# Strassen products of an FFN input: two of four weight sums made by an adding transfer, with signs that turn all sums into additions

## The chip, the cores and the metric

The kernel runs on one core of a Trainium2 chip (trn2). The metric is the device time of one execution in microseconds. Five engines work side by side, each through its own queue in order: TensorE (PE; PEld is its weight load), VectorE (DVE), ScalarE (ACT), GpSimd (POOL) and SyncE (SP), which only issues transfers here.

## The reference

One inference step of a four-layer decoder for 512 prompt tokens and 8 sample tokens, held together as T = 520 columns of a model width of 1024. Each layer is a token mixer (sparse attention, chunked gating, linear recurrence, sparse attention) and then a dense SwiGLU network, both with a normalized residual:

```python
def swiglu_ffn(x, w_in, w_out):
    gate, up = jnp.split(x @ w_in, 2, axis=-1)
    return (jax.nn.silu(gate) * up) @ w_out
...
xp = deepnorm(xp, swiglu_ffn(xp, ffn_w_in[layer], ffn_w_out[layer]), ln_gain[layer, 1], ln_bias[layer, 1])
```

The hidden width is 2816 = 22 blocks of 128; each block has a gate part and an up part in w_in. Everything is float32.

## The kernel before, in words

**Matrix products.** x lies transposed in SBUF, 128 rows by 8 blocks (k) by 520 columns. A float32 product is made of three passes with split operands: each operand is rounded to a high part H (a CAST on ScalarE) and the residue is kept as L (a subtraction, mostly on VectorE); TensorE adds H x H, L x H and H x L into one PSUM bank. For weights `Weights.split` does this: the cast at L145, the residue at L147. A step of `Weights` is one such split of a 128 x 512 piece. `need` keeps the steps five ahead of the product that asks for one (`ahead`), and with `lag` set, as in the FFN, a residue is issued only with the next step's cast. Engines run strictly in the order in which the kernel issues their instructions.

**The FFN.** The 22 hidden blocks are taken in three chunks of 8, 7 and 7 (`CH`). In `ffn_body` the first 3 blocks of the first chunk are plain products (`mm`, L330 to L332); the other 5, and all of the next chunks, are Strassen pairs. After each chunk `out_proj` multiplies the gated hidden rows by w_out.

**A Strassen pair.** A pair is the gate block and the up block of one hidden block: A11 and A12 are the two halves of the gate weights (k 0 to 3 and 4 to 7), A21 and A22 those of the up weights. B11 to B22 are the corresponding quarters of x (260 columns each). Seven products of 12 matmuls (`prod`, L523 to L525) replace eight:

```python
PRODUCTS = (("A11", "B11", 0), ("S1", "T1", 1), ("S2", "T2", 3), ("A12", "B21", 4), ("S4", "B22", 5),
            ("S3", "T3", 6), ("A22", "T4", 9))
```

The third number places the product in the order of all pairs of the chunk, seven apart from pair to pair. The sums of a pair are S1 = A21 + A22, S2 = S1 - A11, S3 = A11 - A21, S4 = A12 - S2. All four run on GpSimd (`sum`: S1 at L170, S2 at L172, S3 at L174, S4 at L176), four steps ahead of the split that reads them (`SUMLEAD`), into five rotating buffers called fsum.

**The other side.** `right` makes T1 = B12 - B11, T2 = B22 - T1, T3 = B22 - B12 and T4 = B21 - T2 once per layer, in two halves (j = 0, 1), all at L502: T1 and T2 on VectorE, T3 and T4 on GpSimd. Each is then split by `Net.split` (L291 cast, L292 residue). They share the fsum buffers with the weight sums. This happens while TensorE still runs the plain products.

**Taking the products apart.** `gated` collects the seven products in three PSUM banks per pair (x: products 0, 2, 5, 6; y: 1, 4; z: 3). Products 0, 1, 2 and 5 are copied out by ScalarE (L570), and a later product into the same bank waits for that copy. VectorE adds 3 and 4 (L573, L576) and multiplies 6 (L583); GpSimd adds and multiplies the up part (L579, L580; in a chunk's last pair VectorE does); ScalarE applies SiLU (L550) and casts (L555), VectorE takes the residue (L556).

**Transfers.** SP loads each pair with two transfers of 512 KB (`dma`, L131), as soon as slots of the common pool of 39 (g) come free, at most some steps ahead. The normalization before the FFN (`ln`) ends with eight tensor_scalar of GpSimd per half of the columns (L397) and the residues L353 of VectorE that wait for them. It runs while TensorE is in the plain products, and its GpSimd instructions are issued between the first weight sums.

## Time and profile before

| what | us |
|---|---|
| median of 3 runs | 3063.47 (3060.45 to 3068.73) |
| the profiled execution, its time | 3060.67 |
| the profiled execution, its span | 3059.0 |
| TensorE busy | 2798.2 |
| VectorE busy | 2201.5 |
| ScalarE busy | 1538.7 |
| GpSimd busy | 1106.8 |

The profile is that of one execution. Busy times are sums over the span; a row of the trace gives an instruction's start, length, engine, source line, operation and tiles (out<-in), and in brackets how long its engine had idled before it and what ended that. Matmuls overlap each other, so what one costs is the distance of two starts, not the length of one. PEclk is the share of the full TensorE clock that was granted.

### The profile page before, as it was taken

To read this page: it belongs to the slowest core of one execution; us is meant where nothing else is said; L and a number is where in the kernel's file an instruction comes from. 1 tells how busy PE (TensorE), PEld (TensorE's weight loads), DVE (VectorE), ACT (ScalarE), POOL (GpSimd) and SP (SyncE) were. 2 spreads that over 40 slices of the span, in tenths; PEclk is the share of its full clock that TensorE was granted. 3 is DMA by queue.
4 is the path that set the end of the run, shared out by engine and by line. 5 is a ranking of instruction groups with operands and counts; after the bars stand their busy time and mean duration, and the time that the engine had idled before them with its cause. 6 is when DMAs were issued, how large, how long until landed. Compare 5 with 4: busy or idle time off the path is not lost.

```text
span 3059.0 us, 56135 instructions
## 1 busy us (share of the span) xinstructions
PE 2798.2 (91%) x21818; PEld 2663.7 (87%) x21818; DVE 2201.5 (72%) x4197; ACT 1538.7 (50%) x3466; POOL 1106.8 (36%) x894
## 2 busy tenths in 40 slices
PE   7999888999989889998899898999899988889997
PEld 7888578999989889998899888999898876889997
DVE  4788656686856786687677677587768877575885
ACT  4666544454445453464445445354456665353543
POOL 0222144364431454354222226355312222353562
PEclk9999999999999999999999999999999999999999
DMA  4222541333323032341212221332322144313321
GB/s 173 65 61 83 162 141 50 97 98 103 97 77 111 29 97 83 103 133 63 78 57 78 71 98 56 98 103 88 115 85 65 58 126 153 108 59 102 96 94 53
DMA packets 136044, 280.59 MB, mean 92 GB/s; under 512 B 13026, under 2 KB 76002, under 8 KB 135778
## 3 DMA queue, kind: packets, MB, share of 16 engines
q1 hardware_dynamic: 127168, 261.86, 26.9%
q10 hardware_dynamic: 7458, 10.95, 1.0%
q0 software_dynamic: 1152, 4.19, 0.5%
q8 instruction: 172, 2.82, 0.4%
q14 instruction: 94, 0.77, 0.1%
HBM read 263.69 MB, written 13.27 MB: 91 GB/s over the span
## 4 chain that ended last, share of the span: by engine, by line
PE 58%; DVE 16%; ACT 7%; issue 3%; POOL 3%; DMA 1%; SPq 0%; ACTq 0%; POOLq 0%; DVEq 0%
PE ps L330 9%; PE ps L332 9%; PE ps L331 9%; PE ps L523 8%; PE ps L525 7%; PE ps L524 7%; DVE g L147 3%; DVE row L375 2%; POOL x L397 2%; PE ps L846 1%; DVE x L366 1%; ACT g L291 1%; DVE g L828 1%; DVE g L292 1%; ACT g L1155 1%
## 5 line engine op out<-in xcount | busy, mean ns | idle before, releaser
L330 PE MATMUL ps<-g 128*128 128x256 f32 (+1 forms) x3744 | 1100.4, 294 | 21.4 <-ACT g L145 13.9
L331 PE MATMUL ps<-g 128*128 128x256 f32 (+1 forms) x3744 | 1073.1, 287 | 23.3 <-DVE g L147 20.6
L332 PE MATMUL ps<-g 128*128 128x256 f32 (+1 forms) x3744 | 1073.3, 287 | 2.9 <-DVE g L353 1.6
L330 PEld LDWEIGHTS ps<-g 128*128 128x128 f32 x3744 | 723.9, 193 | 34.7 <-ACT g L145 14.1
L331 PEld LDWEIGHTS ps<-g 128*128 128x128 f32 x3744 | 723.1, 193 | 31.6 <-DVE g L147 22.8
L332 PEld LDWEIGHTS ps<-g 128*128 128x128 f32 x3744 | 720.6, 192 | 4.3 <-DVE g L292 2.3
L523 PE MATMUL ps<-g 128*128 128x260 f32 x2128 | 608.6, 286 | 47.2 <-ACT frow L570 47.2
L524 PE MATMUL ps<-g 128*128 128x260 f32 x2128 | 604.6, 284 | 0.0
L525 PE MATMUL ps<-g 128*128 128x260 f32 x2128 | 604.2, 284 | 0.0
L147 DVE TENSOR_TENSOR g<-g 128x512 fp32r<-128x512 f32 (+1 forms) x632 | 497.3, 806 | 79.8 <-ACT g L145 79.0
L145 ACT CAST g<-g 128x512 fp32r<-128x512 f32 (+1 forms) x712 | 418.6, 610 | 156.7 <-PE ps L332 111.1
L523 PEld LDWEIGHTS ps<-g 128*128 128x128 f32 x2128 | 404.5, 190 | 53.8 <-ACT frow L570 53.8
L524 PEld LDWEIGHTS ps<-g 128*128 128x128 f32 x2128 | 404.9, 190 | 0.0
L525 PEld LDWEIGHTS ps<-g 128*128 128x128 f32 x2128 | 404.8, 190 | 0.0
L147 DVE TENSOR_TENSOR g<-fsum,g 128x512 fp32r<-128x512 f32 x304 | 346.4, 1157 | 23.6 <-ACT g L145 20.0
L145 ACT CAST g<-fsum 128x512 fp32r<-128x512 f32 x304 | 189.0, 623 | 56.9 <-PE ps L332 48.7
L1155 ACT ACTIVATE g<-g,nst 128x128 f32<-128x128 f32 (+3 forms) x256 | 143.4, 561 | 120.5 <-DVE nst L1153 118.5
L1167 POOL TENSOR_SCALAR g<-g,nst 128x128 f32<-128x128 f32 (+3 forms) x64 | 76.4, 1194 | 344.1 <-DVE nst L1160 236.4
L147 POOL TENSOR_TENSOR g<-g 128x512 fp32r<-128x512 f32 x80 | 105.7, 1327 | 250.4 <-ACT g L145 244.5
L170 POOL TENSOR_TENSOR fsum<-g 128x512 f32<-128x512 f32 x76 | 120.8, 1590 | 148.3 <-DMA g<-ffn_in 129.5
L172 POOL TENSOR_TENSOR fsum<-fsum,g 128x512 f32<-128x512 f32 x76 | 123.8, 1629 | 127.3 <-issue 126.1
L570 ACT COPY frow<-ps 128x260 f32<-128x260 f32 x304 | 113.7, 374 | 110.3 <-PE ps L525 110.3
(268 smaller groups left out, 4341.8 us busy)
## 6 DMA issues: line engine op xcount, KB each, us to landing
g<-ffn_in SPq DMA_DIRECT2D x176, 512.0 KB, 4.1
g<-ffn_out SPq DMA_DIRECT2D x64, 448.0 KB, 3.3
g<-nsa_in SPq DMA_DIRECT2D x42, 512.0 KB, 4.2
cm<-cache_cmp SPq DMA_DIRECT2D x64, 256.0 KB, 3.7
g<-cache_slc SPq DMA_DIRECT2D x128, 128.0 KB, 2.4
g<-cache_win SPq DMA_DIRECT2D x32, 512.0 KB, 4.8
...
```

The lines of the kernel that those rows point to most:

```text
L145: self.nc.scalar.copy(h, src)
L147: self.subs.append(lambda: (eng or self.nc.vector).tensor_sub(l, src, h.bitcast(FT)))
L170: g.tensor_add(t, q(2, 1), q(2, 2))
L172: g.tensor_sub(t, self.sums[i, "S1"], q(1, 1))
L330: nc.tensor.matmul(p[:, :n], H[:, s], a, start=k == 0, stop=False)
L331: nc.tensor.matmul(p[:, :n], L[:, s], a, start=False, stop=False)
L332: nc.tensor.matmul(p[:, :n], H[:, s], b, start=False, stop=k == nk - 1)
L523: nc.tensor.matmul(p, H[:, s], a, start=start and k == 0, stop=False, skip_group_check=True)
L524: nc.tensor.matmul(p, L[:, s], a, start=False, stop=False, skip_group_check=True)
L525: nc.tensor.matmul(p, H[:, s], b, start=False, stop=k == 3, skip_group_check=True)
L570: nc.scalar.copy(s[q], p)
L1155: defer(lambda P=P, i=i: (self.table(LN_EXP), nc.scalar.activation(P, P, AF.Exp, bias=st[:, i:i + 1], scale=-1.0, accum_out=st[:, 4 + i:5 ...
```

## The change

Four things, all in the FFN input.

1. **Signs.** T1, T2 and T4 are now B11 - B12, -(T1 + B22) and -(T2 + B21); T3 stays. The weight sums become S1 = A21 + A22, S3 = A21 + A11, S2 = S1 + A11 and S4 = S2 + A12 in the terms of the new layout: the up weights lie first in memory, then the gate weights, which gives quarters 0 to 3 = (A21, A22, A11, A12) of one row of 2048 numbers. The host's arrangement of ffn_w_in changes accordingly; the signs that differ are taken up where the products come out (L577 with scale -1 for products 1 and 5, a factor -1 for product 6).
2. **S1 and S3 by transfers.** `begin` at "D" lets SP load quarter 0 (A21) twice, side by side, into one slot. At "add" GpSimd issues a transfer that adds quarters 1 and 2 (A22, A11) onto it. The halves of the slot then are S1 and S3. "A1" loads quarters 2 and 3 (A11, A12) and "A22" loads quarter 1 again, into an fsum buffer.
3. **S2 and S4** stay on GpSimd, as additions (L180).
4. **T2 and T4** become SCALAR_TENSOR_TENSOR on VectorE; T4 thereby leaves GpSimd.

The lead of each part, in steps, is in LEADS: the load D is issued 12 steps ahead of S1's split, the addition 7, A1 6 ahead of A11's, A22 5, S2 and S4 3. Lines from `Weights` on move by 6 or 7 (L502 becomes L503 to L509, L523 to L525 become L530 to L532, L570 becomes L577, L579 and L580 become L586 and L587).

```diff
--- before.py
+++ after.py
@@ -39,7 +39,8 @@
 
 PRODUCTS = (("A11", "B11", 0), ("S1", "T1", 1), ("S2", "T2", 3), ("A12", "B21", 4), ("S4", "B22", 5),
             ("S3", "T3", 6), ("A22", "T4", 9))
-SUMLEAD = 4
+
+LEADS = (("D", "S1", 12), ("add", "S1", 7), ("A1", "A11", 6), ("S2", "S2", 3), ("S4", "S4", 3), ("A22", "A22", 5))
 HALF = T // 2
 
 
@@ -87,7 +88,8 @@
 
     def __init__(self, net):
         self.net, self.nc = net, net.nc
-        self.items, self.raw, self.ready, self.sums = [], {}, {}, {}
+        self.items, self.raw, self.ready = [], {}, {}
+        self.pairs, self.got = [], {}
         self.steps, self.pos, self.first, self.early = [], {}, [], {}
         self.nd = self.n = 0
         self.rawn, self.ahead = 3, 5
@@ -107,18 +109,16 @@
 
     def plan_pairs(self, pairs):
 
-        i0 = len(self.items)
-        self.items += pairs
+
+        i0 = len(self.pairs)
+        self.pairs += pairs
         for n, q in products(len(pairs)):
-            key = i0 + n, PRODUCTS[q][0]
+            key = ("p", i0 + n), PRODUCTS[q][0]
             self.add(key, lambda key=key: self.factor(*key))
-        for i in range(i0, len(self.items)):
-            for x in ("S1", "S2", "S4", "S3"):
-                at = self.pos[i, x] - SUMLEAD
-                self.early.setdefault(at, []).append((i, x))
-                if x == "S1":
-                    self.first.append(at)
-        return list(range(i0, len(self.items)))
+        for i in range(i0, len(self.pairs)):
+            for x, of, lead in LEADS:
+                self.early.setdefault(max(0, self.pos[("p", i), of] - lead), []).append((i, x))
+        return [("p", i) for i in range(i0, len(self.pairs))]
 
     def add(self, key, f):
         self.pos[key] = len(self.steps)
@@ -158,36 +158,36 @@
         n = self.items[i][0].shape[1]
         self.split((i, p), self.taken(i)[0][:, 512 * p:min(n, 512 * p + 512)], self.sub[p])
 
...
+
+    def begin(self, i, x):
+
+        nc, ap, t = self.nc, self.pairs[i], self.got.setdefault(i, {})
+        if x == "D":
+            d = self.net.flat(FT)[:, :1024]
+            nc.sync.dma_start(d.rearrange("p (a b) -> p a b", a=2), ap[:, None, :512].to_broadcast([128, 2, 512]))
+            t["S1"], t["S3"], t["D"] = d[:, :512], d[:, 512:], d
+        elif x == "add":
+            nc.gpsimd.dma_start(t["D"], ap[:, 512:1536], accum_op=OP.add)
+        elif x == "A1":
+            r = self.net.flat(FT)[:, :1024]
+            nc.sync.dma_start(r, ap[:, 1024:])
+            t["A11"], t["A12"] = r[:, :512], r[:, 512:]
+        elif x == "A22":
+            t[x] = self.net.fsum()
+            nc.sync.dma_start(t[x], ap[:, 512:1024])
         else:
...
+            t[x] = self.net.fsum()
+            p, q = ("S1", "A11") if x == "S2" else ("S2", "A12")
+            nc.gpsimd.tensor_add(t[x], t[p], t[q])
+
+    def factor(self, u, name):
+        self.split((u, name), self.got[u[1]][name], None)
 
     def need(self, *key):
 
         lim = min(len(self.steps), self.pos[key] + 1 + self.ahead)
         while self.n < lim:
             for x in self.early.pop(self.n, ()):
-                self.sum(*x)
+                self.begin(*x)
             self.steps[self.n][1]()
             self.n += 1
         if self.n == len(self.steps):
@@ -476,9 +476,10 @@
         u, j0 = [], 0
         f = lambda ap: ap.rearrange("p k c -> p (k c)")
         for c, n in enumerate(CH):
-            pairs = [tuple(f(a["ffn_in"][layer, j, s]) for s in range(2)) for j in range(j0, j0 + n)]
+            pairs = [a["ffn_in"][layer, j].rearrange("p s k c -> p (s k c)") for j in range(j0, j0 + n)]
             m = PLAIN if c == 0 else 0
-            u.append((self.W.plan([x for pair in pairs[:m] for x in pair]), self.W.plan_pairs(pairs[m:])))
+            plain = [x[:, s:s + 1024] for x in pairs[:m] for s in (1024, 0)]
+            u.append((self.W.plan(plain), self.W.plan_pairs(pairs[m:])))
             u.append(self.W.plan([f(a["ffn_out"][layer, m, :, j0:j0 + n]) for m in range(8)]))
             j0 += n
         return u
@@ -489,17 +490,23 @@
     def right(self, X, B):
 
 
-        nc = self.nc
+        v, g = self.nc.vector, self.nc.gpsimd
         x = lambda r, c, j: self.x[:, 4 * r - 4 + 2 * j:4 * r - 2 + 2 * j, HALF * (c - 1):HALF * c]
         for n in ("T1", "T2", "T3", "T4"):
             B[n] = [self.flat(FR)[:, :4 * HALF].rearrange("p (k t) -> p k t", k=4) for _ in range(2)]
         for j in range(2):
             t = {}
-            for n, o, p, q in (("T1", nc.vector, x(1, 2, j), x(1, 1, j)), ("T2", nc.vector, x(2, 2, j), "T1"),
-                               ("T3", nc.gpsimd, x(2, 2, j), x(1, 2, j)), ("T4", nc.gpsimd, x(2, 1, j), "T2")):
+            for n in ("T1", "T2", "T3", "T4"):
                 t[n] = self.fp.tile([128, HALF * 2], FT, name="fsum", tag="fsum", bufs=5).rearrange(
                     "p (k t) -> p k t", k=2)
-                o.tensor_sub(t[n], t.get(p, p) if isinstance(p, str) else p, t[q] if isinstance(q, str) else q)
+                if n == "T1":
+                    v.tensor_sub(t[n], x(1, 1, j), x(1, 2, j))
+                elif n == "T2":
+                    v.scalar_tensor_tensor(t[n], t["T1"], -1.0, x(2, 2, j), op0=OP.mult, op1=OP.subtract)
+                elif n == "T3":
+                    g.tensor_sub(t[n], x(2, 2, j), x(1, 2, j))
+                else:
+                    v.scalar_tensor_tensor(t[n], t["T2"], -1.0, x(2, 1, j), op0=OP.mult, op1=OP.subtract)
                 self.split(B[n][0][:, 2 * j:2 * j + 2], B[n][1][:, 2 * j:2 * j + 2], t[n])
                 yield
         for r, c in ((1, 1), (2, 1), (2, 2)):
@@ -567,7 +574,7 @@
             run_due()
             if q in (0, 1, 2, 5):
                 s[q] = self.frow()
-                nc.scalar.copy(s[q], p)
+                nc.scalar.activation(s[q], p, AF.Copy, scale=-1.0 if q in (1, 5) else 1.0)
             eng = nc.vector if last else nc.gpsimd
             if q == 3:
                 nc.vector.tensor_add(s[0], s[0], p)
@@ -580,7 +587,7 @@
                 defer(2, lambda s=s, e=eng: e.tensor_mul(s[1], s[1], s[2]))
                 put(3, j, 1, s[1])
             elif q == 6:
-                nc.vector.tensor_mul(s[0], s[0], p)
+                nc.vector.scalar_tensor_tensor(s[0], p, -1.0, s[0], op0=OP.mult, op1=OP.mult)
                 put(1, j, 0, s[0])
         while due:
             run_due()
@@ -1530,7 +1537,8 @@
     g = np.concatenate([i["ln_gain"].reshape(8, 8, 128), i["gmlp_ln_v"][:, 0].reshape(1, 8, 128)], 0)
     b = np.concatenate([i["ln_bias"].reshape(8, 8, 128), i["gmlp_ln_v"][:, 1].reshape(1, 8, 128)], 0)
     o["ln_gb"] = np.stack([g, b], 1).transpose(3, 0, 1, 2)
-    o["ffn_in"] = i["ffn_w_in"].reshape(DEPTH, 8, 128, 2, NFF, 128).transpose(0, 4, 3, 2, 1, 5)
+    o["ffn_in"] = i["ffn_w_in"].reshape(DEPTH, 8, 128, 2, NFF, 128)[:, :, :, ::-1].transpose(
+        0, 4, 2, 3, 1, 5)
     o["ffn_out"] = i["ffn_w_out"].reshape(DEPTH, NFF, 128, 8, 128).transpose(0, 3, 2, 1, 4)
     blocks = lambda w: w.reshape(8, 128, -1, 128).transpose(2, 1, 0, 3)
     o["gmlp_in"], o["gmlp_out"] = blocks(i["gmlp_w_in"][0]), blocks(i["gmlp_w_out"][0])
```

On GpSimd, in mid-stretch, in the seven-product rhythm of one pair. Before (fsum is a weight sum, frow an evicted product):

```order
L170 TENSOR_TENSOR fsum<-g 128x512
L579 TENSOR_TENSOR frow<-frow 128x260
L172 TENSOR_TENSOR fsum<-fsum,g 128x512
L580 TENSOR_TENSOR frow<-frow 128x260
L176 TENSOR_TENSOR fsum<-g,fsum 128x512
L174 TENSOR_TENSOR fsum<-g 128x512
```

And now:

```order
L180 TENSOR_TENSOR fsum<-g 128x512
L169 DMA g<-ffn_in 128x1024
L180 TENSOR_TENSOR fsum<-fsum,g 128x512
L586 TENSOR_TENSOR frow<-frow 128x260
L587 TENSOR_TENSOR frow<-frow 128x260
```

Four sums became two, and the adding transfer (L169) of the next pair stands between S2 and S4 of this one.

On VectorE, in one pass of `right` (g<-fsum is the residue of a T). Before:

```order
L502 TENSOR_TENSOR fsum<-x 128x520
L292 TENSOR_TENSOR g<-fsum,g 128x520
L502 TENSOR_TENSOR fsum<-x,fsum 128x520
L292 TENSOR_TENSOR g<-fsum,g 128x520 x3
L617 TENSOR_TENSOR row<-row,ps 128x264
```

And now:

```order
L503 TENSOR_TENSOR fsum<-x 128x520
L292 TENSOR_TENSOR g<-fsum,g 128x520
L505 SCALAR_TENSOR_TENSOR fsum<-fsum,x 128x520
L292 TENSOR_TENSOR g<-fsum,g 128x520 x2
L509 SCALAR_TENSOR_TENSOR fsum<-fsum,x 128x520
L292 TENSOR_TENSOR g<-fsum,g 128x520
L624 TENSOR_TENSOR row<-row,ps 128x264
```

T4 (L509) now stands on VectorE between the residue of T3 and its own.

On GpSimd at the start of a layer's FFN, among the last instructions of the normalization (L397). Before:

```order
L170 TENSOR_TENSOR fsum<-g 128x512
L172 TENSOR_TENSOR fsum<-fsum,g 128x512
L397 TENSOR_SCALAR x<-x,lngn,lngb 128x264 x8
L176 TENSOR_TENSOR fsum<-g,fsum 128x512
L174 TENSOR_TENSOR fsum<-g 128x512
L170 TENSOR_TENSOR fsum<-g 128x512
L502 TENSOR_TENSOR fsum<-x 128x520
L502 TENSOR_TENSOR fsum<-x,fsum 128x520
```

And now:

```order
L169 DMA g<-ffn_in 128x1024
L397 TENSOR_SCALAR x<-x,lngn,lngb 128x264 x4
L180 TENSOR_TENSOR fsum<-g 128x512
L397 TENSOR_SCALAR x<-x,lngn,lngb 128x264 x4
L169 DMA g<-ffn_in 128x1024
L180 TENSOR_TENSOR fsum<-fsum,g 128x512
L507 TENSOR_TENSOR fsum<-x 128x520 x2
```

The first pair's S2 stands between the two halves of the eight L397, and T4 is gone from this queue; only the two T3 (L507) are left of `right`.

## Rows read from the trace of the kernel before

**Rows 1.** The page, part 1: busy time, share of the span, instructions.

```profile
PE 2798.2 (91%) x21818; PEld 2663.7 (87%) x21818; DVE 2201.5 (72%) x4197; ACT 1538.7 (50%) x3466; POOL 1106.8 (36%) x894
```

**Rows 2.** The page, part 4: the chain that ended last, by engine.

```profile
PE 58%; DVE 16%; ACT 7%; issue 3%; POOL 3%; DMA 1%; SPq 0%; ACTq 0%; POOLq 0%; DVEq 0%
```

**Rows 3.** Windows: length, busy PE, PEld, DVE, ACT, POOL (count), clock, DMA share, GB/s.

```profile
620.00:640.00 20.00, 20.00 (x169) 20.00 (x168) 15.86 (x21) 12.67 (x30) 12.46 (x10) 1.00 0.34 116
650.00:670.00 20.00, 19.46 (x162) 19.25 (x162) 19.93 (x21) 10.47 (x26) 16.51 (x12) 1.00 0.18 51
```

**Rows 4.** Timeline of TensorE, the three restarts in the stretch from 617.7 to 691.0.

```profile
660.12 0.39 PE L523 MATMUL ps<-g 128*128 128x260 f32 x1 [0.54 <-ACT frow L570]
...
671.19 0.39 PE L523 MATMUL ps<-g 128*128 128x260 f32 x1 [0.72 <-ACT frow L570]
...
689.27 0.39 PE L523 MATMUL ps<-g 128*128 128x260 f32 x1 [0.52 <-ACT frow L570]
```

**Rows 5.** Groups from 649.08 to 671.2: count, busy us, mean ns, idle before.

```profile
L147 DVE TENSOR_TENSOR g<-fsum,g 128x512 fp32r<-128x512 f32 x8 | 10.5, 1330 | 0.1
...
L170 POOL TENSOR_TENSOR fsum<-g 128x512 f32<-128x512 f32 x2 | 3.5, 1736 | 0.0
L174 POOL TENSOR_TENSOR fsum<-g 128x512 f32<-128x512 f32 x2 | 2.9, 1471 | 0.0
```

**Rows 6.** Timeline of VectorE at 648 us, where GpSimd idles.

```profile
647.87 0.41 DVE L576 TENSOR_TENSOR frow<-frow,ps 128x260 f32<-128x260 f32 x1
648.21 0.68 DVE L147 TENSOR_TENSOR g<-fsum,g 128x512 fp32r<-128x512 f32 x1
```

**Rows 7.** Waits of TensorE over the span: us, times, longest.

```profile
PE ps L523 <- ACT frow L570: 47.2, 32, 9.3
```

**Rows 8.** Timeline of VectorE, GpSimd and TensorE before layer 0's 5-pair stretch.

```profile
499.46 0.70 DVE L502 TENSOR_TENSOR fsum<-x 128x520 f32<-128x520 f32 x1
...
507.09 0.70 DVE L292 TENSOR_TENSOR g<-fsum,g 128x520 fp32r<-128x520 f32 x1 [2.08 <-ACT g L291]
...
508.96 0.69 DVE L502 TENSOR_TENSOR fsum<-x 128x520 f32<-128x520 f32 x1
510.35 0.70 DVE L292 TENSOR_TENSOR g<-fsum,g 128x520 fp32r<-128x520 f32 x1 [0.69 <-ACT g L291]
...
512.36 2.18 DVE L292 TENSOR_TENSOR g<-fsum,g 128x520 fp32r<-128x520 f32 x2 [0.70 <-ACT g L291]
516.60 1.21 DVE L292 TENSOR_TENSOR g<-fsum,g 128x520 fp32r<-128x520 f32 x1 [2.05 <-ACT g L291]
...
514.62 1.28 POOL L502 TENSOR_TENSOR fsum<-x,fsum 128x520 f32<-128x520 f32 x1 [1.48 <-DVE g L292]
...
521.13 0.58 PE L523 MATMUL ps<-g 128*128 128x260 f32 x1 [6.57 <-ACT frow L570]
```

**Rows 9.** Tile hgrn_state, loads of 512 KB that GpSimd issues: time to landing.

```profile
DMA to landing us min/median/max: 4.3/5.5/7.1
```

**Rows 10.** Timeline of GpSimd and VectorE at one such issue.

```profile
1471.60 0.93 POOL L925 DMA_DIRECT2D g<-hgrn_state  x1 [8.34 <-ACT g L145]
...
1471.53 0.69 DVE L147 TENSOR_TENSOR g<-g 128x512 fp32r<-128x512 f32 x1
```

**Rows 11.** Lines 432 and 434, plain and signed form: ns min/median/max.

```profile
L432 DVE TENSOR_TENSOR row<-row x34: 415/428/806, 449.9 to 3049.6; 128x256 f32<-128x256 f32 x17, 128x264 f32<-128x264 f32 x17
...
L434 DVE SCALAR_TENSOR_TENSOR row<-row x34: 418/426/434, 450.4 to 3050.0; 128x256 f32<-128x256 f32 x17, 128x264 f32<-128x264 f32 x17
```

**Rows 12.** Windows behind the pauses of 3.20 and of 6.57 us; columns as above.

```profile
491.20:497.00 5.80, 5.80 (x35) 5.80 (x36) 4.92 (x5) 3.50 (x8) 4.76 (x4) 0.71 0.02 4
521.10:531.00 9.90, 9.87 (x63) 9.87 (x64) 7.46 (x10) 5.01 (x12) 4.40 (x4) 0.74 0.17 50
```

**Rows 13.** Timeline of GpSimd and TensorE at the normalization's end in layer 0.

```profile
487.62 3.95 POOL L397 TENSOR_SCALAR x<-x,lngn,lngb 128x264 f32<-128x264 f32 x4 [0.39 <-ACT g L393]
...
491.19 0.39 PE L331 MATMUL ps<-g 128*128 128x256 f32 x1 [3.20 <-DVE g L147]
```

19 lines of the change are left out of this document (removed).

## Prediction

> **What bounds the kernel now.** I read the page first: TensorE is busy 91% of the span, VectorE 72%, GpSimd 36% [rows 1], and the chain that ended last is 58% TensorE, 16% VectorE and 3% GpSimd [rows 2]. So time is to be had only where TensorE stands still, and the change touches only the stretches of the Strassen products. There are 12: per layer one of 5 pairs and two of 7. A pair is 7 products of 12 matmuls, 84 in all.
>
> Next I laid two windows of 20 us in one 7-pair stretch side by side [rows 3]. In the early one TensorE starts 169 matmuls, one per 0.12 us, and VectorE is busy 15.86 us; in the later one TensorE starts 162 and VectorE is busy 19.93 us. A pair costs TensorE 84 x 0.12 = 10.08 us. Late in the stretch TensorE stands still twice, and restarts at 660.12 and 671.19 [rows 4]: the period of a pair is 11.07 us there, and VectorE is busy through all of it. VectorE sets the pace once the lead of the first pairs is eaten. TensorE idles 0.54 and 0.72 us for ScalarE's copy L570, which comes late because ScalarE first waits for VectorE's eviction L573. The third wait, 0.52 us at 689.27, is of another sort: in the last pair the product with S3 is followed at once by the one with A22 in the same bank, and the copy lies between them.
>
> Why VectorE is late shows in the groups of two such periods [rows 5]: the residue L147 of a sum takes 1330 ns on average. Where GpSimd idles the same instruction takes 0.68 us, and an eviction before it 0.41 us, of which 0.07 overlaps with what follows [rows 6]. So, undisturbed, a pair would cost VectorE 7 residues x 0.61 + 5 operations of the eviction's width (L573, L576, L583, twice L556) x 0.34 = 5.97 us. The other 11.07 - 5.97 = 5.1 us fall on GpSimd's work, 16.51 us in 20 [rows 3], that is 9.1 per period: 0.56 us of VectorE per us of GpSimd.
>
> Last I took all waits of TensorE on L570: 47.2 us in 32 waits, the longest 9.3 [rows 7]. The 24 in the eight 7-pair stretches, 1.8 us a stretch as in [rows 4], make 14.4; some 32 us lie in the four 5-pair stretches, nearly all of it at one place, before the first product with S2 (6.57 us in layer 0 [rows 8]).
>
> **The change part by part.**
>
> *Two sums fewer on GpSimd.* S1 and S3 (L170 and L174, 1.74 + 1.47 us [rows 5]) become the work of a transfer. GpSimd keeps 9.1 - 3.2 = 5.9 us per pair, which at 0.56 cost VectorE 3.3 us: a pair takes it 5.97 + 3.3 = 9.3 us, or 9.8 if issuing the adding transfer (0.93 us [rows 10]) disturbs it like a sum. The bounds 5.97 and 9.8 both lie under TensorE's 10.08. So the two waits in mid-stretch go; next in line is TensorE itself. Each costs its idle time, plus 0.16 (a matmul is drawn 0.28 long but starts every 0.12), plus 0.11 (the one that restarts is drawn 0.39): 0.54 + 0.72 + 0.54 = 1.8 us per 7-pair stretch, in eight of them **-14.4 us**. The third wait stays.
>
> *T4 from GpSimd to VectorE.* Ahead of the 5-pair stretch VectorE and ScalarE work through T1 to T4 twice [rows 8]. The first pass runs from 499.46 to 507.09 + 0.70 = 507.79, 8.33 us; the second from 508.96 to 516.60 + 1.21 = 517.81, 8.85. GpSimd's T4 starts only when VectorE has finished T3's residue, and its 1.28 us lie in the chain. Afterwards GpSimd makes only T3, from x alone, which I take to be ready in time. From T1 to T2's residue 3.40 us remain (512.36 - 508.96). Then come the residues of T2 and T3, 2 x 0.63; T4 and its cast until its residue starts, 1.39 like T1's (510.35 - 508.96), since the signed form costs what the plain one does (426 against 428 ns, [rows 11]); and that residue, 0.70: 6.75 us. Saved are 1.6 + 2.1 = 3.7 us per layer. The tail from there to TensorE's restart at 521.13 is untouched, so TensorE restarts that much sooner: **-15 us** over four layers.
>
> *The clock behind that pause.* After the 6.57 us the granted clock averages 0.74 over 9.9 us, a mix of its two levels, 1.2 and 2.4 GHz: 2.6 us lost. After a pause of 3.20 us it is 0.71 over 5.8 us: 1.7 lost [rows 12]. The pause that remains is 6.57 - 3.7 = 2.9 us, so I take the nearer row: **-3.6 us** over four layers. Bounds: 0 and, with no loss left, -10.4.
>
> *S2 of the first pair, moved on GpSimd.* It now stands between the two halves of the eight L397. The later half started at 487.62 after 0.39 us of idling [rows 13], so it comes 1.28 - 0.39 = 0.9 us later (a sum like T4's 1.28). TensorE's 3.20 us pause there, behind an L147 that stands behind the L353 that waits for L397, grows as much. I price it at nothing: the T chain, not TensorE, decides the restart. Without that cover it costs 4 us over the layers.
>
> *The transfers.* SP issues three per pair instead of two, GpSimd one; 1.75 MB land instead of 1, so the DMA share of 0.34 [rows 3] would become some 0.6. D, A1 and A22 are issued pairs (over 10 us) ahead of their use and hide. SP's new wait, for a free sum buffer, holds up the next D and A1, which have that lead too. On GpSimd the adding transfer waits for D, and the next S2 waits until the addition has landed; S4, L579 and L580 are queued behind, and ScalarE's casts wait for them. A round there is landing + a sum 1.74 + issue 0.93. The trace has no adding transfer. Copies issued by GpSimd land in 4.3 to 7.1 us, median 5.5 [rows 9]. Lower bound 5.5, a copy; upper bound 11, twice that, since source and destination are both read. I take 7.1, the slowest copy: a round of 9.8, under 10.08, no cost.
> A rule speaks against this transfer: by the Trainium skill, SBUF — State Buffer, section "SBUF: two separate sides", GpSimd cannot write a transfer's descriptors while VectorE runs a two-port copy, and one of about 0.62 us became 3.1. With 2.5 us more on a landing of 5.5 a round would be 10.7 us, an estimate; over five rounds that is 3 us, within the lead worked out below, so the sum would stay. The trace does not show such a stall: an issue took 0.93 us while VectorE ran a residue, which kept its 0.69 [rows 10].
>
> *Signs.* L570 gets a scale and L583 a factor, with the same operands and widths: no cost [rows 11].
>
> **Sum.** -14.4 - 15 - 3.6 = -33. The profiled execution took 3060.67 us, 2.8 under the median of the runs, 3063.47. That makes 3027.7 on its scale and 3030.5 on the median's. Forecast: **3030 us**, its own range 3018 to 3042.
>
> **Rivals.**
> 1. *The additions land late*, and the change ends slower. With 11 us a round is 13.7, 3.6 us over TensorE's pair. A 7-pair stretch has five such rounds, 18 us, of which some 5 are covered (weights are prepared five products, 7.2 us, ahead; cast and residue take 2): 13 lost instead of 1.8. A 5-pair one has three: 11 less 5, 6 lost against 4.6 won. Together 8 x 11.2 + 4 x 1.4 = +95: 3158. It turns into a loss from about 9 us of landing. For it: no row has such a transfer; against it: the copies' rows. 0.10.
> 2. *VectorE stays over 10.08 us*, because the issue holds it or GpSimd's remaining work costs it more: only the T chain's 18.6 us are won, 3045. 0.12.
> 3. *The starting pause stays*, behind T3 or something else, and the longer pause of the normalization is paid: -14.4 + 4, 3053. 0.10.
> 4. *Nothing moves*: 2 and 3 together, 3063. For it: GpSimd is 3% of the chain. 0.08.
>
> **Chances.** The forecast has 0.60. A measurement of this kernel can tell 0.3%, 9 us, from no change. Faster: forecast, 2 and 3, 0.82. Same: 4, 0.08. Slower: 1, 0.10. The range leaves out 1 and 4 (0.18). It reaches from the whole clock loss won back and two more us per layer, 3014, to rival 3, 3053.
>
> **What would show it.** Right: a late window of 20 us in a 7-pair stretch holds 167 to 169 matmuls, with VectorE clearly under 20 us; L147 on a sum is under 1.0 us; TensorE's waits on the copy are about 0.5 us per 7-pair stretch and some 3 at the start of a 5-pair one; T1 to T4's residue takes near 6.7 us, twice. Wrong: GpSimd waits of several us for the transfer, landings of 9 us or more, or VectorE still full.

## The result and the profile after

| | before | after |
|---|---|---|
| median, us | 3061.96 (3058.99 to 3068.73, 4 runs) | 3026.73 (3025.43 to 3028.20, 4 runs) |
| span of the profiled execution, us | 3059.0 | 3024.5 |

The ratio is 0.9882 (95% interval 0.9864 to 0.9900). The medians lie 35 us apart, forecast 33. The time is inside the likeliest case's own range. Of the three terms, the profile bears out the one of GpSimd's sums with its cause, and that of the clock in its sum only. The third, the move of T4, has about the right sum for a reason that the runs refute.

The page, part 1, and the chain by engine. VectorE lost 169 us of work and GpSimd 220 [rows 1], and TensorE now holds 69% of the chain instead of 58% [rows 2]:

```profile
PE 2796.2 (92%) x21818; PEld 2663.4 (88%) x21818; DVE 2032.7 (67%) x4205; ACT 1554.8 (51%) x3466; POOL 887.0 (29%) x810
...
PE 69%; DVE 16%; ACT 7%; issue 3%; DMA 2%; POOL 2%; SPq 1%; ACTq 0%; POOLq 0%; DVEq 0%
```

Two windows late in a 7-pair stretch, and the groups of two pairs there (columns as in [rows 3, 5]):

```profile
640.00:660.00 20.00, 20.00 (x169) 20.00 (x168) 15.70 (x25) 13.31 (x31) 11.51 (x10) 1.00 0.62 143
650.00:670.00 20.00, 20.00 (x170) 20.00 (x169) 15.42 (x25) 13.71 (x31) 10.65 (x9) 1.00 0.54 147
```

```profile
L147 DVE TENSOR_TENSOR g<-g 128x512 fp32r<-128x512 f32 x8 | 8.6, 1080 | 1.1 <-ACT g L145 1.1
L147 DVE TENSOR_TENSOR g<-fsum,g 128x512 fp32r<-128x512 f32 x7 | 5.1, 723 | 0.7 <-ACT g L145 0.7
...
L180 POOL TENSOR_TENSOR fsum<-g 128x512 f32<-128x512 f32 x2 | 3.6, 1812 | 0.0
...
L180 POOL TENSOR_TENSOR fsum<-fsum,g 128x512 f32<-128x512 f32 x2 | 3.2, 1602 | 0.0
...
L587 POOL TENSOR_TENSOR frow<-frow 128x260 f32<-128x260 f32 x2 | 2.2, 1079 | 0.2
...
L563 DVE TENSOR_TENSOR g<-frow,g 128x260 fp32r<-128x260 f32 x4 | 1.7, 418 | 0.0
...
L586 POOL TENSOR_TENSOR frow<-frow 128x260 f32<-128x260 f32 x2 | 1.5, 747 | 8.4 <-ACT frow L577 8.4
```

TensorE starts 169 or 170 matmuls in 20 us where it started 162, VectorE is busy 15.4 to 15.7 us instead of 19.93, and GpSimd's four instructions take 1.81 + 1.60 + 1.08 + 0.75 = 5.24 us per pair, ahead of which it idles for 4.2.

The two groups of L147 cannot be compared by name, because S1 and S3 now lie in a slot g and A22 in a buffer fsum. In the kernel before, the window of [rows 5] also has these residues:

```profile
L556 DVE TENSOR_TENSOR g<-frow,g 128x260 fp32r<-128x260 f32 x4 | 6.1, 1514 | 0.0
...
L147 DVE TENSOR_TENSOR g<-g 128x512 fp32r<-128x512 f32 x7 | 5.2, 741 | 0.0
```

All weight residues together fell from a mean of 1055 ns ((8 x 1330 + 7 x 741) / 15) to 913, which is 1.0 us per pair of seven. The residue of the gated rows (L556, now L563), two per pair, fell from 1514 to 418 ns, which is 2.2 us. So two thirds of what VectorE won lie in a residue that the prediction did not name as slowed.

Both mid-stretch waits are gone: a 7-pair stretch, from its first matmul to the end of its last, takes 71.2 to 71.5 us in all eight instead of 73.2 or 73.3.

TensorE's waits on ScalarE's copy over the span (47.2 us in 32 before, [rows 7]):

```profile
PE ps L530 <- ACT frow L577: 17.5, 16, 5.0
```

Twelve of the 16 are the last-pair wait. The others stand ahead of the first product with S2, one per layer. In layer 0 the timeline of VectorE, GpSimd and TensorE shows the T chain that leads up to it (compare [rows 8]):

```profile
498.12 0.69 DVE L503 TENSOR_TENSOR fsum<-x 128x520 f32<-128x520 f32 x1
...
501.51 1.31 DVE L292 TENSOR_TENSOR g<-fsum,g 128x520 fp32r<-128x520 f32 x2 [0.69 <-ACT g L291]
502.74 0.69 DVE L509 SCALAR_TENSOR_TENSOR fsum<-fsum,x 128x520 f32<-128x520 f32 x1
504.18 0.70 DVE L292 TENSOR_TENSOR g<-fsum,g 128x520 fp32r<-128x520 f32 x1 [0.75 <-ACT g L291]
...
506.49 0.69 DVE L503 TENSOR_TENSOR fsum<-x 128x520 f32<-128x520 f32 x1
...
512.50 1.02 DVE L292 TENSOR_TENSOR g<-fsum,g 128x520 fp32r<-128x520 f32 x1 [0.70 <-ACT g L291]
...
496.29 1.63 POOL L507 TENSOR_TENSOR fsum<-x 128x520 f32<-128x520 f32 x1 [2.25 <-DVE g L147]
504.96 1.31 POOL L507 TENSOR_TENSOR fsum<-x 128x520 f32<-128x520 f32 x1 [7.04 <-DVE g L292]
...
517.02 0.39 PE L530 MATMUL ps<-g 128*128 128x260 f32 x1 [2.06 <-ACT frow L577]
```

The passes take 6.76 us (498.12 to 504.88) and 7.03 (506.49 to 513.52), forecast 6.75 each. T3 (L507) now starts before T1, at 496.29. The residues of T2 and T3 take 1.31 us together; before they took 2.16 there, and 2.18 in the second pass.

The clock behind the start pauses of the four layers, columns as above:

```profile
517.00:526.90 9.90, 9.88 (x82) 9.88 (x83) 6.97 (x11) 6.79 (x16) 3.26 (x4) 1.00 0.58 179
1073.60:1083.50 9.90, 9.83 (x59) 9.83 (x60) 4.88 (x10) 4.98 (x12) 0.60 (x1) 0.69 0.25 74
1853.10:1863.00 9.90, 9.90 (x70) 9.90 (x71) 5.47 (x10) 5.78 (x13) 1.79 (x3) 0.83 0.57 177
2685.40:2695.30 9.90, 9.87 (x82) 9.87 (x83) 7.02 (x11) 6.80 (x16) 3.29 (x4) 1.00 0.56 177
```

In layers 0 and 3 all of the 9.9 us run at the full clock of 2.4 GHz (1.00), behind pauses of 2.06 and 1.97 us; the same stretches before held 63 and 62 matmuls. In layers 1 and 2, behind pauses of 4.95 and 2.13 us, the clock averages 0.69 and 0.83, a mix with the lower level, and nothing was won (60 and 71 matmuls before).

The adding transfer, line L169: its issue on GpSimd in ns (min/median/max) and its time to landing:

```profile
L169 POOL DMA_DIRECT2D g<-ffn_in x76: 829/868/1043, 465.2 to 2934.1; - x76
...
DMA to landing us min/median/max: 5.3/5.9/10.6
```

### The profile page after: what moved, and what is told of

Its sections match the earlier page's. It is cut to its first block, busy times and chain, and to the rows that moved or that the text cites. A ratio compares the mean times of both kernels' runs of the same rounds, so it can differ in the third digit from the quotient of the medians.

```text
span 3024.5 us, 56356 instructions
## 1 busy us (share of the span) xinstructions
PE 2796.2 (92%) x21818; PEld 2663.4 (88%) x21818; DVE 2032.7 (67%) x4205; ACT 1554.8 (51%) x3466; POOL 887.0 (29%) x810
## 3 DMA queue, kind: packets, MB, share of 16 engines
HBM read 323.46 MB, written 13.27 MB: 111 GB/s over the span
## 4 chain that ended last, share of the span: by engine, by line
PE 69%; DVE 16%; ACT 7%; issue 3%; DMA 2%; POOL 2%; SPq 1%; ACTq 0%; POOLq 0%; DVEq 0%
PE ps L330 11%; PE ps L332 11%; PE ps L331 11%; PE ps L530 8%; PE ps L531 8%; PE ps L532 8%; DVE row L375 2%; PE ps L853 1%; DVE g L147 1%; PE ps L1032 1%; ACT g L1162 1%; PE ps L1209 1%; PE ps L1158 1%; DVE g L1160 1%; POOL x L397 1%
## 5 line engine op out<-in xcount | busy, mean ns | idle before, releaser
L331 PE MATMUL ps<-g 128*128 128x256 f32 (+1 forms) x3744 | 1075.0, 287 | 27.8 <-DVE g L147 25.1
L331 PEld LDWEIGHTS ps<-g 128*128 128x128 f32 x3744 | 724.4, 193 | 36.0 <-DVE g L147 27.3
L147 DVE TENSOR_TENSOR g<-g 128x512 fp32r<-128x512 f32 x708 | 588.6, 851 | 121.2 <-ACT g L145 120.3
L530 PE MATMUL ps<-g 128*128 128x260 f32 x2128 | 604.3, 284 | 17.5 <-ACT frow L577 17.5
L532 PE MATMUL ps<-g 128*128 128x260 f32 x2128 | 602.8, 283 | 0.0
L145 ACT CAST g<-g 128x512 fp32r<-128x512 f32 (+1 forms) x788 | 462.1, 607 | 139.6 <-PE ps L332 78.4
L530 PEld LDWEIGHTS ps<-g 128*128 128x128 f32 x2128 | 402.7, 189 | 20.9 <-ACT frow L577 20.9
L532 PEld LDWEIGHTS ps<-g 128*128 128x128 f32 x2128 | 402.8, 189 | 0.0
L577 ACT ACTIVATE frow<-ps 128x260 f32<-128x260 f32 x304 | 118.0, 388 | 247.2 <-PE ps L532 247.2
L147 DVE TENSOR_TENSOR g<-fsum,g 128x512 fp32r<-128x512 f32 x228 | 165.1, 724 | 38.6 <-ACT g L145 38.6
L147 POOL TENSOR_TENSOR g<-g 128x512 fp32r<-128x512 f32 x80 | 105.7, 1328 | 250.1 <-ACT g L145 250.1
L586 POOL TENSOR_TENSOR frow<-frow 128x260 f32<-128x260 f32 x64 | 47.9, 748 | 430.5 <-ACT frow L577 430.5
L180 POOL TENSOR_TENSOR fsum<-g 128x512 f32<-128x512 f32 x76 | 121.0, 1593 | 132.0 <-DMA g<-ffn_in 112.1
L145 ACT CAST g<-fsum 128x512 fp32r<-128x512 f32 x228 | 133.9, 616 | 41.2 <-PE ps L332 41.2
```

Source lines behind the costliest of these rows:

```text
L145: self.nc.scalar.copy(h, src)
L147: self.subs.append(lambda: (eng or self.nc.vector).tensor_sub(l, src, h.bitcast(FT)))
L180: nc.gpsimd.tensor_add(t[x], t[p], t[q])
L331: nc.tensor.matmul(p[:, :n], L[:, s], a, start=False, stop=False)
L530: nc.tensor.matmul(p, H[:, s], a, start=start and k == 0, stop=False, skip_group_check=True)
L532: nc.tensor.matmul(p, H[:, s], b, start=False, stop=k == 3, skip_group_check=True)
```

## The experiments

Each ran beside the kernel before on the same chip. The medians of the kernel before lie between 3059.20 and 3062.49 us there, so rows are compared by their ratios. The last three columns are those of the one profiled execution, which for the kernel named all took 3019.72 us, 11 over its median. The wait column is the sum of TensorE's waits on the copy of a product (L570, L577 or the line that an edit makes of it) over the span; passes are T1's start to the end of T4's residue in layer 0; a stretch is one of 7 pairs.

| kernel | median us | ratio to before (95%) | wait us | passes us | stretch us |
|---|---|---|---|---|---|
| before | 3061.96 | | 47.2 | 8.33, 8.84 | 73.2 |
| after | 3026.73 | 0.9882 (0.9864 to 0.9900) | 17.5 | 6.76, 7.03 | 71.4 |
| t4_alone | 3056.26 | 0.9981 (0.9971 to 0.9991) | 44.4 | 7.73, 8.36 | 73.2 |
| sums_alone | 3022.01 | 0.9864 (0.9845 to 0.9884) | 14.3 | 5.92, 7.05 | 71.4 |
| load_back | 3089.53 | 1.0085 (1.0066 to 1.0104) | 59.9 | 6.75, 7.03 | 76.8 |
| late_add | 3027.54 | 0.9888 (0.9869 to 0.9907) | 18.3 | 6.76, 7.02 | 71.4 |
| more_bufs | 3056.40 | 0.9993 (0.9983 to 1.0004) | 40.2 | 5.97, 8.11 | 73.2 |
| t4_pool | 3017.66 | 0.9861 (0.9846 to 0.9876) | 12.1 | 5.93, 7.05 | 71.4 |
| s2_behind | 3025.58 | 0.9884 (0.9869 to 0.9899) | 23.8 | 6.76, 7.00 | 71.4 |
| last_pair | 3017.98 | 0.9868 (0.9851 to 0.9885) | 9.8 | as after | 70.5 |
| no_s13 | 3024.56 | 0.9881 (0.9866 to 0.9896) | 17.2 | 5.97, 8.12 | 71.4 |
| both | 3009.59 | 0.9837 (0.9824 to 0.9851) | 6.5 | 5.93, 7.05 | 70.5 |
| all | 3008.40 | 0.9831 (0.9817 to 0.9844) | 13.9 | 6.92, 7.28 | 70.5 |
| lag_dve | 3006.50 | 0.9814 (0.9801 to 0.9828) | 2.7 | 13.1 for both | 70.5 |

### T4 moved alone, and the sums moved alone

```diff
-  ... ("T4", nc.gpsimd, x(2, 1, j), "T2")):
+  ... ("T4", nc.vector, x(2, 1, j), "T2")):
```

> The kernel before with one edit: T4 is subtracted on VectorE instead of GpSimd; the four weight sums, the loads and all signs stay as before. Theory (the parts add up: T4 sets the pause ahead of a 5-pair stretch, GpSimd's sums set the waits in mid-stretch): each pass of T1 to T4 takes 6.75 us instead of 8.33 and 8.85, the pause before the first product with S2 shrinks by some 4 us in each layer, less time runs at the low clock behind it, the 7-pair stretches stay at 73.2 us: 15 + 4 = 19 us less than before, 3043. Rival A (GpSimd's four sums per pair hold the start as well, so T4 alone wins nothing): no change, 3062. Rival B (the sums matter only at the start, and T4's place carries most of the whole gain): 7-pair stretches go to 71.4 us here too, 30 us or more less than before.

Measured 3056.26, 6 us less than before, not 19. A pass lost 0.6 and 0.5 us, not 1.6 and 2.1. The timeline of layer 3 in this kernel (GpSimd's T3, VectorE's residues of T2 and T3) shows why:

```profile
2690.54 1.31 POOL L502 TENSOR_TENSOR fsum<-x 128x520 f32<-128x520 f32 x1 [6.35 <-DVE fsum L502]
...
2691.09 2.16 DVE L292 TENSOR_TENSOR g<-fsum,g 128x520 fp32r<-128x520 f32 x2 [0.69 <-ACT g L291]
```

T3 reads only x, yet it starts when VectorE has finished T2's addition, and so runs beside T2's residue; the two residues take 2.16 us, where they take 1.31 in the changed kernel. The kernel before has the same wait ahead of T3:

```profile
2693.58 1.31 POOL L502 TENSOR_TENSOR fsum<-x 128x520 f32<-128x520 f32 x1 [6.34 <-DVE fsum L502]
```

And T4, now VectorE's, starts at 2693.28, right behind T3's residue, where GpSimd's T4 started too. Neither my theory nor a rival had this.

The changed kernel with T4 back on GpSimd:

```diff
-  v.scalar_tensor_tensor(t[n], t["T2"], -1.0, x(2, 1, j), op0=OP.mult, op1=OP.subtract)
+  g.tensor_add(t[n], t["T2"], x(2, 1, j))
```

> The changed kernel with T4 made by GpSimd again, as T2 + B21; its sign is then the opposite of the changed kernel's, so the products with T4 come out with the wrong sign. The adding transfer, the two remaining sums and the order stay as changed. Theory (the parts add up): the 7-pair stretches stay at 71.4 us, the pause before the first product with S2 is back at 6 to 9 us with the low clock behind it: 15 us less than before, 3047, 20 us more than the changed kernel. Rival A (with two sums fewer GpSimd reaches T4 sooner, and the pause stays short): within 6 us of the changed kernel, 3027 to 3033. Rival B (the 7-pair stretches gained by T4's place in the queues, not by the sums): 73 us per 7-pair stretch again.

Measured 3022.01: rival A, and more than it said, though the intervals of this ratio and of the change's overlap. Layer 3 in the timeline (GpSimd's T4, VectorE's three residues from T2's on):

```profile
2666.20 1.31 POOL L509 TENSOR_TENSOR fsum<-fsum,x 128x520 f32<-128x520 f32 x1 [3.04 <-DVE fsum L505]
...
2666.75 2.54 DVE L292 TENSOR_TENSOR g<-fsum,g 128x520 fp32r<-128x520 f32 x3 [0.69 <-ACT g L291]
```

With T3 out of the way T4 runs on GpSimd beside T2's residue and out of the chain's way. A first pass takes 5.92 us; T4 on VectorE adds 0.84. So the time came from the two sums, at the start too. This kernel has the new leads and loads as well; no_s13, below, leaves only the two sums out and has T3 early too.

### Why T3 was late

```diff
-SLOTS = 39
+SLOTS = 38
-  ... name="fsum", tag="fsum", bufs=5) ...
+  ... name="fsum", tag="fsum", bufs=7) ...
```

> The kernel before with seven fsum buffers instead of five (and 38 slots of the common pool instead of 39, which makes the room); the four sums, T3 and T4 stay on GpSimd. Theory (in the kernel before three of the five fsum buffers are held by pending weight sums, so T3 takes T1's buffer and waits until VectorE has read T1 for T2; T3 then runs beside the residues, which stretch, and T4 queues behind it): T3 starts before T1 is made, T4 runs right behind T2's addition and is hidden, a pass of T1 to T4 takes 6 to 7 us instead of 8.3 and 8.8, the pause before the first product with S2 shrinks by some 4 us a layer with less low clock behind it, the 7-pair stretches stay at 73.2 us: 15 to 20 us less than before, 3042 to 3047. Rival (GpSimd's own load by the weight sums at the start makes the pause, not the buffers): T3 may start early, but the pause stays within 1 us of the one before, 3057 to 3064.

The first pass fell to 5.97 us, with T3 before T1 and T4 right behind T2's addition: the buffers did hold T3, and T4 as well. The pause fell by 1.0 to 2.1 us, between the theory and the rival. But the time is unclear, 0.9993, and the second pass stayed at 8.11. Layer 3, GpSimd and VectorE:

```profile
2685.62 1.63 POOL L502 TENSOR_TENSOR fsum<-x 128x520 f32<-128x520 f32 x1 [1.30 <-DVE g L147]
2691.81 1.31 POOL L502 TENSOR_TENSOR fsum<-x,fsum 128x520 f32<-128x520 f32 x1 [4.56 <-DVE fsum L502]
...
2692.39 2.51 DVE L292 TENSOR_TENSOR g<-fsum,g 128x520 fp32r<-128x520 f32 x3 [0.75 <-ACT g L291]
...
2700.39 1.75 POOL L172 TENSOR_TENSOR fsum<-fsum,g 128x512 f32<-128x512 f32 x1
2702.22 1.61 POOL L176 TENSOR_TENSOR fsum<-g,fsum 128x512 f32<-128x512 f32 x1
...
2699.67 4.72 DVE L292 TENSOR_TENSOR g<-fsum,g 128x520 fp32r<-128x520 f32 x3 [0.69 <-ACT g L291]
```

The weight sums of the next pair stand behind T4 on GpSimd. With T4 early they start beside the second pass, and its three residues take 4.72 us, where those of the first pass take 2.51. So buffers alone move the collision into the second pass. The waits on the copy fell by 7.0 us and the time by less; one slot fewer in the common pool may cost something, which was not separated.

### GpSimd's load put back, and the transfer taken away

```diff
   nc.gpsimd.tensor_add(t[x], t[p], t[q])
+  nc.gpsimd.tensor_add(t[x], t[p], t[q])
```

> The changed kernel with S2 and S4 each added twice by GpSimd into the same buffer, so that GpSimd makes four sums per pair as before, while S1 and S3 still come by transfer. Theory (what cost time was GpSimd's load beside VectorE): VectorE, at 15.4 to 15.9 us in 20 in the changed kernel, goes to 19 us or more in 20 late in a 7-pair stretch, the two waits on the copy in mid-stretch come back, and the 7-pair stretches take about 73 us: some 14 us more than the changed kernel, 3041. Rival A (each us of GpSimd costs VectorE 0.37 us, as the changed kernel's 7.9 us per pair against 5.97 undisturbed with 5.2 of GpSimd would have it, so VectorE comes to 9.2 us and stays under TensorE's 10.08): no waits, within 5 us of the changed kernel. Rival B (it was the place of S1 and S3 in the order, not the load): within 5 us too, but with VectorE under 17 us in 20.

The theory held and its size did not: 63 us more than the changed kernel, not 14. The window at 650 us:

```profile
650.00:670.00 20.00, 18.53 (x153) 18.32 (x154) 19.87 (x20) 11.10 (x26) 17.16 (x14) 1.00 0.51 116
```

VectorE is full again with 20 instructions, and a stretch takes 76.8 us, longer than before the change: GpSimd now makes four sums and issues the transfer. The residue of the gated rows is back at 1512 ns (window 660.2 to 683.6). Rival A's price of 0.37 us is refuted.

```diff
+  if name in ("S1", "S3"):
+      self.sums[i, name] = q(2, 1) if name == "S1" else q(1, 1)
+      return
```

> The kernel before without the sums S1 and S3: the products that should have them get A21 and A11, unsummed, in their place (S2 is then A21 - A11). GpSimd makes S2 and S4 only, as in the changed kernel, but there is no adding transfer, no second load of A21 and A22, and T3 and T4 stay on GpSimd. Theory (the whole gain is that GpSimd makes two sums fewer, and the transfer that takes them over costs nothing): as the changed kernel with T4 on GpSimd, 3015 to 3020; 7-pair stretches of 71.4 us, passes of T1 to T4 of 6 and 7 us. Rival A (the transfer has a price: 15 MB more per layer, its issue on GpSimd): 3010 or less, with 7-pair stretches still at 71.4 us. Rival B (the new leads and the order on the queues carry part of the gain): above 3025.

Measured 3024.56, a ratio of 0.9881, where the change has 0.9882; stretches of 71.4 us. Leaving the two sums out gives what the transfer gives, with VectorE less busy than the 15.70 us of the changed kernel:

```profile
640.00:660.00 20.00, 20.00 (x170) 20.00 (x169) 14.80 (x25) 13.41 (x30) 9.75 (x8) 1.00 0.26 76
```

So the transfer, with 60 MB more read from HBM (323.46 against 263.69), costs no time that shows. The median lies 5 us above the theory's range. The second pass stays at 8.12 us, as in more_bufs: S2 and S4 stand right behind T4, and the three residues beside them take 4.75 us in layer 3. In sums_alone S2 starts 0.69 us after T4 and they take 3.63. Fewer sums alone thus clear the first pass and not the second, and whether the second pass is the whole difference from the theory's range was not separated.

### Does it matter when the addition lands?

```diff
-... ("add", "S1", 7), ...
+... ("add", "S1", 3), ...
```

> The changed kernel with one number changed: the adding transfer is issued three steps ahead of S1's split instead of seven, so on GpSimd it stands behind S4 and not between S2 and S4, and the next S2 comes only two steps later. Theory (landing, then S2, S4, the frow work and the issue follow each other on GpSimd, and this round must stay under TensorE's 10.08 us per pair): 5.9 + 1.6 + 1.6 + 1.8 + 0.9 = 11.8 us, 1.7 over; five rounds lose 8.5 us per 7-pair stretch, of which some 5 are covered by the lead of the weights: 3 to 4 us lost in each of eight, some 30 us more than the changed kernel, 3057; GpSimd waits for the transfer for 2 us or more per pair. Rival (the lead of five steps in the split weights, 7.2 us, covers any such lateness, and the round does not add up because the frow work runs while the transfer lands): within 5 us of the changed kernel, although GpSimd waits for the transfer.

The rival was right: 3027.54, stretches unchanged. GpSimd's timeline:

```profile
641.02 0.73 POOL L586 TENSOR_TENSOR frow<-frow 128x260 f32<-128x260 f32 x1 [4.01 <-ACT frow L577]
...
646.01 0.89 POOL L169 DMA_DIRECT2D g<-ffn_in  x1
651.08 0.74 POOL L586 TENSOR_TENSOR frow<-frow 128x260 f32<-128x260 f32 x1 [4.18 <-ACT frow L577]
...
652.94 1.80 POOL L180 TENSOR_TENSOR fsum<-g 128x512 f32<-128x512 f32 x1
```

Between the issue and the next S2 lie 6.9 us whatever the transfer does, since L586 waits 4.18 us for ScalarE and L587 follows it. A landing of 5.6 us (the median here) hides in that.

### Where else the start and the end of a stretch could give

```diff
   for x, of, lead in LEADS:
+      lead = 2 if i == i0 and x == 'S2' else lead
```

> The changed kernel with the first pair's S2 of each chunk two steps ahead of its split instead of three, so that at the start of a layer it stands on GpSimd behind all eight L397 and not between the halves. Theory (the 0.9 us by which S2 delays the later L397 are not covered: VectorE's whole queue up to T1 stands behind them): the pause before L331 shrinks from 4.5 to 3.5 us in three layers, the clock behind it stays high for longer, T1 starts 0.9 us sooner: 4 to 8 us less than the changed kernel, 3019 to 3023. Rival (as the prediction priced it: T1 to T4 decide the restart, not that pause): within 2 us of the changed kernel.

Again the rival: 3025.58. TensorE's pause before L331 in layer 3 went from 4.30 to 3.20 us, and its waits on the copy grew from 17.5 to 23.8. The T chain decides the restart, as the prediction priced it. In layer 0 the L397 end 1.1 us sooner, but T1 starts 45.1 us after the first L397, where the changed kernel has 44.9; what holds T1 there was not separated.

```diff
-    o = [(7 * i + PRODUCTS[q][2], i, q) for i in range(n) for q in range(7)]
+    at = lambda i, q: {4: 6, 5: 5}.get(q, PRODUCTS[q][2]) if i == n - 1 else PRODUCTS[q][2]
+    o = [(7 * i + at(i, q), i, q) for i in range(n) for q in range(7)]
...
-                defer(2, lambda s=s, e=eng: e.tensor_mul(s[1], s[1], s[2]))
-                put(3, j, 1, s[1])
+                defer(2 + last, lambda s=s, e=eng: e.tensor_mul(s[1], s[1], s[2]))
+                put(3 + last, j, 1, s[1])
```

> The changed kernel with the products with S4 and S3 exchanged in the last pair of each chunk, so that another product lies between S3's and A22's, which use the same bank. Theory (the third wait, 0.58 us in each of twelve stretches, is the copy between two products of the same bank and nothing else): each stretch is 0.58 us shorter, 7 us less than the changed kernel, 3020. Rival (the up part of the last pair is ready later, and the product with w_out behind the stretch waits for it instead): within 2 us of the changed kernel.

As expected in the trace: the twelve last-pair waits are gone, and a stretch takes 70.5 us instead of 71.4. The median, 3017.98, is 9 us under the changed kernel's; by the ratios, whose intervals overlap, it is 4. Only the four waits at the start remain:

```profile
PE ps L531 <- ACT frow L578: 9.8, 4, 4.9
```

### A better version

T4 on GpSimd with the right sign:

```diff
-  v.scalar_tensor_tensor(t[n], t["T2"], -1.0, x(2, 1, j), op0=OP.mult, op1=OP.subtract)
+  g.tensor_add(t[n], t["T2"], x(2, 1, j))
...
+  if neg:
+      self.nc.scalar.activation(h, src, AF.Copy, scale=-1.0)
+      self.nc.vector.scalar_tensor_tensor(l, src, -1.0, h.bitcast(FT), op0=OP.mult, op1=OP.subtract)
+      return
```

> The changed kernel with T4 made by GpSimd as T2 + B21 and its sign taken in by T4's cast (scale -1) and residue (factor -1), so that everything is computed as in the changed kernel. Theory (with T3 early, T4 is hidden behind T2's and T3's residues on GpSimd and costs VectorE 0.7 us per pass when it stands there): the first pass takes 5.9 us instead of 6.75, the pause before the first product with S2 is 1.3 to 1.6 us (4.3 in layer 1) instead of 2.2 (5.1): 4 to 6 us less than the changed kernel, 3021 to 3023. Rival (T4's 15 us of the prediction are real): some 15 us more than the changed kernel, 3042.

3017.66; the intervals of this ratio and of the change's overlap, but the waits on the copy (12.1 us against 17.5) and the first pass (5.93) say the same as sums_alone. With the last pair's exchange on top:

> The changed kernel with two edits together, T4 on GpSimd with its sign in the cast and the residue, and the products with S3 and S4 exchanged in the last pair. Theory (the two gains lie in different places of the chain, the start of a 5-pair stretch and the end of every stretch, and add up): 9 + 9 us less than the changed kernel, 3009. Rival (they overlap, or the low clock takes one back): 3013 to 3018.

3009.59: the gains add up, and the interval, 0.9824 to 0.9851, lies clear of the change's. Two more edits on that, S2 behind L397 and this one, each residue of a T issued behind the next T (in the form that it has in lag_dve),

```diff
+  if late:
+      v.tensor_sub(*late.pop())
+  late.append((l, t[n], h.bitcast(FT)))
```

> The kernel with those two edits and two more: the first pair's S2 behind all eight L397, and each residue of a T issued only behind the next T, so that VectorE makes T2 while ScalarE casts T1. Theory (T1 to T4 still decide the restart, with 1.3 to 3.2 us of pause left, and VectorE idles 0.7 us per T for the cast): a pass takes 5 us instead of 5.9 and 7, the pause before the first product with S2 goes under 1 us, and with that out of the way the earlier L397 counts too: 5 to 10 us less than with the two edits, 2999 to 3004. Rival (the pause is by now held by something else, the evictions and casts of the plain products behind T1 to T4): within 3 us of the two edits alone, 3006 to 3012.

gave 3008.40, no clear gain: GpSimd's T3 and T4 then run beside VectorE's T2 and the residues (in layer 3 the second T2 took 1.71 us instead of 0.69, and both passes took 14.1). Without S2's edit and with T4 on VectorE:

> The changed kernel (T4 on VectorE, S2 where the change put it) with the products with S3 and S4 exchanged in the last pair and each residue of a T issued only behind the next T. Theory (the deferral won nothing in the run with all four edits because T4 on GpSimd then ran beside T3's residue and the next T, and stretched them to 1.7 us): with T4 on VectorE only T3 is left on GpSimd, seven operations of 0.62 us and one wait of 0.7 make a pass of some 5.2 us instead of 5.9, from T1 to the end of T4's residue 12.5 us or less for both passes instead of 14.6, and the time is at or under that of the two edits, 3005 to 3010. Rival (the casts of ScalarE, one per T, are what a pass is made of, and the order on VectorE does not matter): both passes take 14.5 us or more, 3012 to 3018.

3006.50, 55 us under before and the lowest median here, though its interval overlaps those of the kernels both and all. Both passes took 13.1 us (T1 at 2650.05, T4's last residue until 2663.14 in layer 3), between the theory's 12.5 and the rival's 14.5, and the wait on the copy is left in one layer only. Against the kernel all, S2's place differs as well as T4's, so the two are not separated. The second T2 is stretched here too (1.70 us, beside GpSimd's T3), so that T4's place alone makes the difference is argued, not shown.

## Why the prediction was right, and where it was not

**The bound, and two sums fewer on GpSimd: right.** Forecast -14.4 us; the eight 7-pair stretches lost 14.8 together. load_back and no_s13 show the cause, GpSimd's work beside VectorE. The sign "L147 on a sum is under 1.0 us" came true, though most of the relief was in L556. Mis-sized was VectorE's load: 9.3 to 9.8 us per pair forecast, 15.70 x 10.08 / 20 = 7.9 measured. The step "0.56 us of VectorE per us of GpSimd" is not a constant: here it is (7.9 - 5.97) / 5.24 = 0.37, and 0.56 came from a stretch where VectorE always had a residue ready to collide. The timeline of the changed kernel shows what happens where it has not:

```profile
642.73 0.69 DVE L147 TENSOR_TENSOR g<-g 128x512 fp32r<-128x512 f32 x1 [0.55 <-ACT g L145]
...
645.02 2.27 DVE L147 TENSOR_TENSOR g<-g 128x512 fp32r<-128x512 f32 x1
...
642.76 1.82 POOL L180 TENSOR_TENSOR fsum<-g 128x512 f32<-128x512 f32 x1
644.52 0.89 POOL L169 DMA_DIRECT2D g<-ffn_in  x1
645.13 1.61 POOL L180 TENSOR_TENSOR fsum<-fsum,g 128x512 f32<-128x512 f32 x1
```

At 642.73 the residue starts first and keeps its 0.69 us, and the sum takes 1.82 (its shortest is 1.27). At 645.02 GpSimd is in the issue, the sum follows, and the residue (A11's, by the order of the products) takes 2.27, ending 0.55 us behind the sum. The Trainium skill, SBUF — State Buffer, section "SBUF: two separate sides", describes such a loss as a lock that whichever starts first holds for its whole instruction. The first case agrees; in the second the sum's record starts 0.11 us after the residue's, so whether the sum or the issue came first there is not shown. The other six residues of a pair take 0.68 to 0.83 us.

**T4 from GpSimd to VectorE: right in sum, wrong in cause.** The chain from the first L397 of the later half of the columns to the end of T4's residue went from 34.30 to 30.79 us in layer 0, and by 3.5 to 3.6 us in every layer, where I said 3.7, and the restart followed. The step that failed is "GpSimd's T4 starts only when VectorE has finished T3's residue, and its 1.28 us lie in the chain", taken as the ground for the 3.7 us. T4 did start there, but on VectorE it stands at the same place, behind T3's residue, and saves only what VectorE is faster (0.70 us against 1.28). The larger part of the 3.7 us lay elsewhere: the residues of T2 and T3 took 2.16 and 2.18 us instead of 1.31 because T3 was late, and T3 was late because the weight sums held the buffers. T4's move alone shortens that chain by 1.1 us (to 33.2), the sums' move alone by 4.4 (to 29.9), and leaving the two sums out, with nothing else of the change, by 3.9 (to 30.4); T4's place on VectorE then costs 0.9. I took the order of the queues for the cause, where the rows name what released T3 ([6.34 <-DVE fsum L502]). They say the same of T4: in [rows 8] GpSimd idles 1.48 us ahead of it until VectorE has finished a residue that T4 does not read, and with seven buffers T4 starts 0.17 us behind T2's addition. "T3, which I take to be ready in time" came true only through the other part of the change, so the sum of this term is luck.

**The clock: right in sum, not in its spread.** Forecast was -0.9 us in each layer, -3.6 together. Measured are 19 and 20 more matmuls in 9.9 us in layers 0 and 3 and one fewer in each of layers 1 and 2, at 0.12 us each 37 x 0.12 = 4.4. The row of the 3.20 us pause did not carry over: behind 2.06 and 1.97 us nothing was lost, behind 2.13 us in layer 2 as much as behind the 8.02 us before. That the sum fits is in part luck, and no run shows why the layers differ.

**S2 between the L397: right.** The pause grew in three layers (from 3.21 to 4.30 us in layer 3; in layer 0 it shrank from 3.20 to 2.36), and s2_behind shows that the T chain covers it.

**The transfers: right in the price; the round was counted too long.** The landing of 5.9 us lay between the bounds 5.5 and 11 and nearer to a copy; no_s13 shows the price, nothing. The time to landing runs from the start of the issue, so the round "landing + a sum 1.74 + issue 0.93", on which rival 1 rests, counts the issue twice. late_add was expected to put S4 and the frow work into it as well, 11.8 us. But the frow work runs behind GpSimd's wait for ScalarE whether the transfer has landed or not, and 5.6 + 1.80 + 1.30 = 8.7 us (landing, S2, S4) are under 10.08. In the changed kernel 8.3 us lie between an issue (644.52) and the next S2 (652.82), and no S2 starts less than 0.6 us after the landing, so rival 1's loss was not tested. Of the signs of being wrong, GpSimd's waits did show, 112.1 us in 16 before S2, but for the load of A11 and A12 (L172) between two stretches; the kernel before has 129.5 us in 13 before S1. One landing took over 9 us, 10.6 at 465.2, 21 us ahead of the first S2.

The estimate of 2.5 us more per landing was worked out from a rule of the Trainium skill, SBUF — State Buffer, section "SBUF: two separate sides", that GpSimd cannot write a transfer's descriptors while VectorE runs a two-port copy. No run here tests the rule: while the 76 issues run, VectorE executes TENSOR_TENSOR and SCALAR_TENSOR_TENSOR and no copy. The median landing of 5.9 us does not hold such a delay.

The three parts, 14.8 + 4 x 3.5 + 4.4 = 33.2, are close to the span's 34.5.
